# Strictly ordered loads and a new split of the last B matrix in a batched trace-of-product kernel

## The chip, the cores and the metric

The kernel runs on one core of a Trainium2 chip. The profiler's span, from first to last instruction, is 1.7 to 1.8 us shorter than the device time of the same run. Moments such as "at 705.1" are us from the start of the span.

The engines of the core run side by side. In this kernel GpSimd issues the loads, which 16 DMA engines carry out; TensorE transposes and does some products, with its results in a memory called PSUM; VectorE and ScalarE copy and multiply. A pool is a fixed set of buffers, each of which is used again when its last reader is done.

## The reference

```python
def setup_inputs():
    B, N = 8, 2176
    return {"a": np.random.randn(B, N, N).astype(np.float32),
            "b": np.random.randn(B, N, N).astype(np.float32)}

def reference(a, b):
    prod = np.matmul(a, b)
    traces = np.diagonal(prod, axis1=1, axis2=2).sum(axis=-1)
    return traces.astype(np.float32)
```

The trace needs no matrix product: it is the sum over all elements of A transposed times B. Each of the 8 batches is therefore a load of two f32 matrices, a transpose of A and a multiply with a sum. 303 MB are read for eight numbers.

## The kernel before

A matrix has 17 tiles of 128 rows, here simply called rows 0 to 16. A load casts f32 to bf16 on its way and is issued by GpSimd. Loads of four rows are joined in twos, so a batch has two double loads of A, a single one, and the same of B. Double loads share three large buffers, singles two small ones.

```python
    even = [ROWS] * (NT // ROWS) + [1] * (NT % ROWS)
    fine = [4, 4, 4, 2, 1, 1, 1]              # groups of rows of the last B
    LAST_PIECES = [(0, 2), (2, 3), (3, 5)]    # row 16 of the last B comes in three pieces
    stage = ctx.enter_context(tc.tile_pool(name="stage", bufs=3))
    single = ctx.enter_context(tc.tile_pool(name="single", bufs=2))
    ...
    def load(src, start, m, count):
        if m == 1:
            t = single.tile([P, 1, N], bf16, tag="single")
        else:
            t = stage.tile([P, DOUBLE * ROWS, N], bf16, tag="stage")
        ...
        issued = nc.gpsimd.dma_start(out=part, in_=rows)
```

TensorE transposes A into PSUM, ScalarE and VectorE copy it into one large tile `at`, and VectorE multiplies each row of B with its part of `at` and sums along the row, 2.29 us for 2048 columns. In the last batch TensorE takes a part of this: products of 128x128 blocks, summed in PSUM, whose diagonal a multiply with the identity picks out at the very end.

```python
        for start, m, count in joined(b_groups):
            if last and start == N - P:             # row 16 of the last B
                b_t = stage.tile([P, DOUBLE * ROWS, N], bf16, tag="stage")
                row = b_t[:, 0, :]
                for g0, g1 in LAST_PIECES:
                    lo, hi = g0 * WIDE, min(g1 * WIDE, N)
                    nc.gpsimd.dma_start(out=row[:, lo:hi], in_=b[bi, start:start + P, lo:hi])
                ...                                  # split over TensorE and VectorE
                continue
            groups, _ = load(b[bi], start, m, count)
            for start, m, b_t in groups:
                v0 = start // P
                for s in range(m):
                    row = b_t[:, s, :]
                    if last and (m == 1 or s % 2 == 1):
                        half = 2 if m == 1 else 0
                        multiply_on_pe(at, row, v0 + s, half, len(a_groups))
                        if half:
                            on_dve(wide_at(at, v0 + s, 0, half), wide(row, 0, half))
                    else:
                        on_dve(wide_at(at, v0 + s, 0, n_wide), wide(row, 0, n_wide))
                        if last:
                            multiply_on_pe(at, row, v0 + s, n_wide, len(a_groups))
```

The instructions go through a scheduler, which keeps what depends on one another in order but may issue a load ahead of an earlier one whose buffer is not yet free.

## Time and profile before

| | before |
|---|---|
| device time, first three runs | 711.77 us (711.19 to 711.93) |
| span | 709.4 us |
| read from HBM over the span | 427 GB/s |
| VectorE, TensorE, ScalarE busy | 58%, 29%, 28% |
| last piece taken up by TensorE | 705.11 |
| product with the identity (last multiply) | 706.67 |

The page's lines on the DMA engines, the stretches by window and the timeline of the end are shown in the prediction below. How to read them: one digit of the DMA row is a fortieth of the span, 9 standing for 90% busy or more. In a timeline line, the columns are start, duration, engine, source line, operation, what it writes and reads, the count of instructions merged, and in brackets the idle time before it with what ended it.

### The profile page before, as it was taken

How to read it: one execution, taken by the hardware profiler on the slowest of the kernel's cores; microseconds unless marked ns; L12 is line 12 of the kernel's file. 1: busy time of each engine (PE TensorE's matmuls, PEld its weight loads, DVE VectorE, ACT ScalarE, POOL GpSimd, SP SyncE). 2: the span in 40 equal slices, each digit the busy share in tenths (PEclk: the TensorE clock that was granted, in tenths of full speed). 3: DMA queues.
4: the chain of work that ended last, by engine and by line, in shares of the span. 5: the costliest groups of instructions: out<-in, count | busy, mean ns of one | idle time of the engine just before them, and what ended most of it. 6: DMA issues, size and time to landing. Idle time of an engine off the chain costs nothing.

```text
span 709.4 us, 3709 instructions
## 1 busy us (share of the span) xinstructions
PE 206.3 (29%) x1406; PEld 193.0 (27%) x1406; DVE 411.4 (58%) x449; ACT 196.8 (28%) x210; POOL 34.6 (5%) x60
## 2 busy tenths in 40 slices
PE   1542005420065100542006510065100560005655
PEld 0542005410065100541005510065000550005655
DVE  0223996139952399514994259932599335993356
ACT  2443005430064200633006420065200651006610
POOL 1000000000010000100000000000000000000000
PEclk9977557765577655766557665577655775557776
DMA  9999999999999999999999999999999999999996
GB/s 220 220 220 219 206 219 220 219 217 209 219 220 218 217 212 216 220 219 215 212 218 220 218 213 215 215 222 217 215 214 213 225 217 212 215 217 222 219 207 138
DMA packets 11620, 152.32 MB, mean 215 GB/s; under 512 B 850, under 2 KB 1106, under 8 KB 3282
## 3 DMA queue, kind: packets, MB, share of 16 engines
q0 software_dynamic: 11456, 150.97, 100.1%
q1 hardware_dynamic: 146, 1.11, 0.4%
q8 instruction: 11, 0.18, 0.1%
q14 instruction: 7, 0.06, 0.0%
HBM read 303.04 MB, written 0.00 MB: 427 GB/s over the span
## 4 chain that ended last, share of the span: by engine, by line
DMA 56%; DVE 34%; issue 7%; PE 2%; another core or an unknown queue 2%; POOL 0%; DVEq 0%; POOLq 0%
DMA t<-in_b_dram 43%; DVE scratch L122 33%; DMA t<-in_a_dram 13%; PE ps L155 1%; DVE acc L122 0%; DVEq L122 0%; PE ps L176 0%; POOL identity masks.py:199 0%; DVE at L110 0%; POOL identity masks.py:197 0%; PE total L298 0%; DVE result L302 0%; DVE late L122 0%; POOLq L74 0%
## 5 line engine op out<-in xcount | busy, mean ns | idle before, releaser
L122 DVE CUSTOM_DVE_ANT_1 scratch<-at,t 128x2048 bf16<-128x2048 bf16 (+1 forms) x156 | 310.6, 1991 | 74.9 <-DMA t<-in_b_dram 67.7
L112 ACT COPY at<-ps 128x1024 bf16<-128x1024 bf16 x208 | 194.4, 1044 | 474.9 <-PE ps L155 474.5
L155 PE MATMUL ps<-identity,t 128*128 128x128 f32 x1071 | 177.9, 334 | 482.5 <-DVE sums L275 262.7
L155 PEld LDWEIGHTS ps<-identity,t 128*128 128x128 f32 x1071 | 166.2, 213 | 490.8 <-DVE sums L275 311.2
L110 DVE COPY at<-ps 128x1024 bf16<-128x1024 bf16 (+2 forms) x104 | 93.5, 902 | 214.4 <-PE ps L155 196.9
L74 POOL DMA_DIRECT2D t<-in_a_dram x23 | 15.3, 663 | 354.3 <-PE ps L176 156.5
L74 POOL DMA_DIRECT2D t<-in_b_dram x26 | 16.8, 645 | 288.3 <-PE ps L176 147.5
L283 PEld LDWEIGHTS <-at 128*128 128x128 bf16 x153 | 17.1, 122 | 13.3 <-issue 12.7
L283 PE MATMUL trace_ps<-t,at 128*128 128x128 bf16 x144 | 16.7, 293 | 12.3 <-DMA t<-in_b_dram 12.3
L176 PE MATMUL ps<-identity,t 128*128 128x128 bf16 x170 | 16.4, 219 | 4.9 <-DVE at L110 4.8
L176 PEld LDWEIGHTS <-t 128*128 128x128 bf16 x170 | 13.0, 100 | 8.3 <-issue 8.0
L122 DVE DVE_READ_ACCUMULATOR2_ANT acc<- 128x1 f32 x163 | 13.3, 81 | 0.0
L86 DVE CAST t<-words 128x1088 bf16<-128x1088 f32 x1 | 0.7, 726 | 4.8 <-DMA words<-in_a_dram 4.8
L247 POOL DMA_DIRECT2D b_t<-in_b_dram x3 | 1.6, 537 | 16.0 <-DVE acc L122 16.0
L122 DVE CUSTOM_DVE_ANT_0 scratch<-at,t 128x128 bf16<-128x128 bf16 x7 | 2.0, 291 | 0.2
L85 ACT CAST t<-words 128x1088 bf16<-128x1088 f32 x1 | 1.1, 1099 | 3.7 <-DMA words<-in_a_dram 3.7
L122 DVE CUSTOM_DVE_ANT_1 scratch<-at,b_t 128x256 bf16<-128x256 bf16 (+1 forms) x3 | 1.5, 510 | 0.1
L275 DVE TENSOR_REDUCE sums<-acc 128x1 f32<-128x22 f32 (+1 forms) x8 | 1.4, 174 | 0.3
L85 ACT ACT_TABLE_LOAD x1 | 1.3, 1283 | 0.7 <-PEq L321 0.7
L283 PE MATMUL trace_ps<-b_t,at 128*128 128x128 bf16 x9 | 1.3, 284 | 0.4 <-DMA b_t<-in_b_dram 0.4
L298 PE MATMUL total<-late,ones 128*1 128x1 f32 x8 | 0.8, 164 | 0.8 <-DVE late L122 0.8
L298 PEld LDWEIGHTS total<-late,ones 128*1 128x1 f32 x8 | 0.3, 80 | 1.2 <-DVE late L122 1.2
(14 smaller groups left out, 2.7 us busy)
## 6 DMA issues: line engine op xcount, KB each, us to landing
t<-in_a_dram POOLq DMA_DIRECT2D x16, 4352.0 KB, 46.7
t<-in_b_dram POOLq DMA_DIRECT2D x15, 4352.0 KB, 51.5
t<-in_b_dram POOLq DMA_DIRECT2D x9, 544.0 KB, 54.5
t<-in_a_dram POOLq DMA_DIRECT2D x7, 544.0 KB, 53.0
t<-in_b_dram POOLq DMA_DIRECT2D x1, 2176.0 KB, 42.9
words<-in_a_dram SPq DMA_DIRECT2D x1, 1088.0 KB, 4.9
t<-in_b_dram POOLq DMA_DIRECT2D x1, 1088.0 KB, 25.7
b_t<-in_b_dram POOLq DMA_DIRECT2D x1, 256.0 KB, 11.7
```

The lines of the kernel that those rows point to most:

```text
L74: issued = nc.gpsimd.dma_start(out=part, in_=rows)
L85: nc.scalar.copy(out=t[:, 0, :half], in_=plain[:, :half])
L86: nc.vector.tensor_copy(out=t[:, 0, half:], in_=plain[:, half:])
L110: last_copy = nc.vector.tensor_copy(out=dst, in_=src)
L112: nc.scalar.copy(out=dst, in_=src)
L122: nc.vector.tensor_tensor_reduce(out=out, in0=x, in1=y, scale=1.0, scalar=0.0, op0=MUL, op1=ADD, accum_out=acc,)
L155: nc.tensor.transpose(ps[:, n * m + r, :], words[:, r, c0:c0 + step * (P - 1) + 1:step], tiles[f32],)
L176: last_transpose = nc.tensor.transpose(ps16[:, n, r, :], a_t[:, r, c0:c0 + P], tiles[bf16],)
L247: nc.gpsimd.dma_start(out=row[:, lo:hi], in_=b[bi, start:start + P, lo:hi])
L275: nc.vector.reduce_sum(out=tiles["sums"][:, bi:bi + 1], in_=acc[:, :cols], axis=mybir.AxisListType.X)
L283: nc.tensor.matmul(trace_ps, x, y, start=(n == 0), stop=(n == len(pe_work) - 1),)
L298: nc.tensor.matmul(total[:, BATCH - 1:BATCH], tiles["ones"], part, start=(n == 0), stop=(n == len(parts) - 1),)
```

## The change

Its intent: loads land in the order in which they are used, VectorE gets the last B in smaller portions and so starts earlier, TensorE takes four whole rows near the end, and the last tile no longer waits for a large buffer.

```diff
+    PE_ROWS = (11, 12, 13, 15)
-    single = ctx.enter_context(tc.tile_pool(name="single", bufs=2))
+    single = ctx.enter_context(tc.tile_pool(name="single", bufs=3))
+    loaded = []
+    def in_order():
+        return tc.issue_after(loaded[-1].ins) if loaded else nullcontext()
     # in load(), and likewise for the pieces of the last tile:
-        issued = nc.gpsimd.dma_start(out=part, in_=rows)
+        with in_order():
+            issued = nc.gpsimd.dma_start(out=part, in_=rows)
+        loaded.append(issued)
...
-        for start, m, count in joined(b_groups):
+        for start, m, count in ([(*g, 1) for g in b_groups] if last else joined(b_groups)):
             if last and start == N - P:
-                b_t = stage.tile([P, DOUBLE * ROWS, N], bf16, tag="stage")
+                b_t = single.tile([P, 1, N], bf16, tag="single")
...
-                    if last and (m == 1 or s % 2 == 1):
-                        half = 2 if m == 1 else 0
-                        multiply_on_pe(at, row, v0 + s, half, len(a_groups))
-                        if half:
-                            on_dve(wide_at(at, v0 + s, 0, half), wide(row, 0, half))
+                    if last and v0 + s in PE_ROWS:
+                        multiply_on_pe(at, row, v0 + s, 0, len(a_groups))
```

More of the change, by code (lines that the diff above doesn't have):

```diff
@@ L1 @@
 import math
-from contextlib import ExitStack
+from contextlib import ExitStack, nullcontext
 import concourse.bass as bass
@@ L246 @@
                     lo, hi = g0 * WIDE, min(g1 * WIDE, N)
-                    nc.gpsimd.dma_start(out=row[:, lo:hi], in_=b[bi, start:start + P, lo:hi])
+                    with in_order():
+                        loaded.append(nc.gpsimd.dma_start(
+                            out=row[:, lo:hi], in_=b[bi, start:start + P, lo:hi]
+                        ))
                 multiply_on_pe(at, row, v0, 0, 1)
```

## The prediction

> **What bounds the kernel now.** I read the page first: the slices (part 2), the queues and the HBM line, then the stretches by window, then the timeline of the last 50 us.
>
> ```profile
> DMA  9999999999999999999999999999999999999996
> GB/s 220 220 220 219 206 219 220 219 217 209 219 220 218 217 212 216 220 219 215 212 218 220 218 213 215 215 222 217 215 214 213 225 217 212 215 217 222 219 207 138
> ...
> q8 instruction: 11, 0.18, 0.1%
> ...
> HBM read 303.04 MB, written 0.00 MB: 427 GB/s over the span
> ```
>
> The DMA engines are at 90% or more in every slice but the last. The GB/s row counts bytes as written in bf16, half of the f32 bytes read: 427 GB/s of reading is the 215 of the page. All compute engines are far from full (VectorE 58%, TensorE 29%). The bound is the stream of loads; everything else counts only before the stream is full or after its last byte.
>
> ```profile
> core 0: us, PE busy (x) PEld busy (x) DVE busy (x) ACT busy (x) POOL busy (x), PEclk, DMA share, GB/s
> 109.80:197.15 87.35, 23.04 (x153) 21.52 (x153) 54.02 (x59) 24.21 (x26) 3.93 (x7) 0.62 1.02 217
> ...
> 284.54:372.04 87.50, 22.87 (x153) 21.25 (x153) 54.04 (x59) 24.21 (x26) 3.95 (x7) 0.62 1.02 216
> ...
> 692.00:705.10 13.10, 9.12 (x78) 8.76 (x78) 9.69 (x12) 0.00 (x0) 1.51 (x3) 0.61 0.91 181
> 705.10:709.40 4.30, 1.25 (x13) 0.64 (x12) 1.76 (x9) 0.00 (x0) 0.00 (x0) 0.76 0.00 0
> ```
>
> One batch takes 87.4 us with its order of loads either A, A, single (the 109.80 stretch) or A, single, A (the 284.54 stretch): GpSimd's own timeline shows both orders, 87.35 against 87.50. After 705.10 nothing is loaded, and 4.3 us remain.
>
> GpSimd's timeline in the batch before the last, and the whole timeline around the start of the last B:
>
> ```profile
> 614.16 0.70 POOL L74 DMA_DIRECT2D t<-in_a_dram  x1 [26.70 <-DMA t<-in_b_dram]
> 634.62 0.71 POOL L74 DMA_DIRECT2D t<-in_b_dram  x1 [19.76 <-DVE acc L122]
> ```
>
> ```profile
> 675.10 0.36 DVE L110 COPY at<-ps 128x384 bf16<-128x384 bf16 x1 [0.88 <-PE ps L176]
> ...
> 681.89 2.29 DVE L122 CUSTOM_DVE_ANT_1 scratch<-at,t 128x2048 bf16<-128x2048 bf16 x1 [6.42 <-DMA t<-in_b_dram]
> ...
> 691.92 1.59 POOL L247 DMA_DIRECT2D b_t<-in_b_dram  x3 [16.03 <-DVE acc L122]
> ```
>
> And the timeline of the end:
>
> ```profile
> 703.51 1.22 DVE L122 CUSTOM_DVE_ANT_1 scratch<-at,t 128x1024 bf16<-128x1024 bf16 x1
> ...
> 704.86 0.68 DVE L122 CUSTOM_DVE_ANT_1 scratch<-at,b_t 128x512 bf16<-128x512 bf16 x1
> 705.11 0.45 PE L283 MATMUL trace_ps<-b_t,at 128*128 128x128 bf16 x3 [0.41 <-DMA b_t<-in_b_dram]
> ...
> 706.05 0.42 DVE L122 CUSTOM_DVE_ANT_1 scratch<-at,b_t 128x256 bf16<-128x256 bf16 x1
> ...
> 706.67 0.29 DVE L122 CUSTOM_DVE_ANT_0 scratch<-identity,trace_ps 128x128 bf16<-128x128 f32 x1 [0.18 <-DVE late L122]
> ```
>
> Here is the only slack that a change can take. The last piece lands at 705.1 (TensorE starts on it at 705.11 and is done at 705.56), but VectorE is still behind: it works on rows of earlier loads until 704.8, then does its three short products one after the other and reaches the product with the identity, the last real step, at 706.67. TensorE has waited 1.1 us for it.
>
> **What the Trainium skill says.** "DMA: Bandwidth & Descriptors", section "Where 436 GB/s comes from", puts the ceiling of a core's 16 engines at 435.2 GB/s. The trace agrees and shows how near it is: a batch reads 2 x 8 x 2176 x 2176 x 4 / 8 = 37.88 MB in 87.4 us, 433 GB/s. The same page, "Anatomy of one DMA — SWDGE (gpsimd) path", says that DMA engines never wait on semaphores; the issuing sequencer waits, and the engines drain what was queued. So a late issue costs only if the queue runs dry. The trace agrees: GpSimd waits up to 30 us at a time while the DMA row stays at 9. "Runtime: NRT & Kernel Launch", section "Instruction fetch mechanics", says that instructions come in blocks of 16 KiB, 256 instructions, by DMA: the 11 packets with 0.18 MB of q8 fit.
>
> **The change, part by part.**
> (1) Strict order of the loads, with a third small buffer. Comparing the instruction orders of the two kernels: GpSimd's list differs from the fourth batch on, where the single A tile no longer overtakes the second double; no load is added there, and no new wait on a landing of the load before appears. Could the queue run dry? At 614.16 the second A is issued; the second B double has just landed (VectorE starts on it at 614.11), and a B single and an A double are still queued. A double takes (87.4 / 34 rows) x 8 = 20.6 us, a single 2.57: 23 us of work. The single that used to lie there too is 2.6 us of it. Next, B is issued at 634.6 with over 20 us queued. So: 0 us in the middle. At the last batch the second A double lands 2.6 us earlier, as the single now follows it; its transposes (661.3 to about 673.5) and the last copies (675.46) move to about 672.9.
>
> (2) The last B in fours. The first four rows land at about 705.1 - 13 x 2.57 = 671.7, not with the double at 681.8; the others at 682.0, 692.2, then 697.4 (two), 699.9, 702.5 and the pieces at 703.7, 704.3, 705.1. VectorE does rows 0 to 10 and 14, twelve, where it did seven and two halves. Steps of 2.29 us plus the reading of the accumulator, 9.5 us for four (681.89 to 691.39): from 672.9 to 682.4; 682.4 to 691.9; three from 692.3 to 699.4; row 14 from 700.0 to 702.4. It keeps level and is idle when the first piece lands. One more load in the stream: below 0.1 us.
>
> (3) Four full rows on TensorE. Matmuls of L283 fall from 153 to 89 (4 x 17, 12 ends of the other rows, 9 of the last). Row 15 lands at 702.5; 17 at 0.114 us (8.21 / 72) end at 704.5, the first piece's four at 705.0, two more at 705.2, the last three at 705.6: as before.
>
> (4) The last tile in the small pool. Its pieces no longer wait for the first double (691.92); in their place they queue behind the two-row load, which waits for the first four rows to be read, about 682.5. Ten us of loads are then still queued, as there were in the kernel before. Gain 0, since the pieces' turn in the stream is the same.
>
> The end: products of the pieces at 703.8 to 704.5, 704.5 to 705.0, and the last at 705.2 to 705.7; the product with the identity, after TensorE at 705.6 and VectorE at 705.7, starts at about 705.85 in place of 706.67. **Sum: -0.8 us**, all behind the last landing. 711.77 - 0.8 = 711.0; I take 710.9, as the program also shrinks by 128 TensorE instructions, half a fetched block, which uses a DMA engine.
>
> **Rivals.**
> (a) Strict order makes a new stall: the second A and the single behind it, both waiting for VectorE, starve the stream. For it: GpSimd waits 26.7 us there, in order, so one late buffer holds all loads behind it. Against: 23 us are queued, and the second and third batches already run in that order at 87.35 us. Losing 3 us in each of five batches would give 726.
> (b) VectorE becomes the bound of the end: 9.5 us for four rows against 10.3 us of loading is a thin margin. If its start stays at 675.5, it ends the third group at 701.8 and row 14 at 704.2; then the pieces' products end 0.5 us late and nearly all is lost: 711.6. A reader should note that it does more work at the end, yet earlier.
> (c) The 16 DMA engines don't end together: in the last 13.1 us the share is 0.91 and the rate 181, where 1.02 and 217 are usual, about 1.4 us per engine on the mean. If a fetch or a changed order falls on another engine, the last landing moves by some tenths, up to 1 us either way: 710 to 712.
> (d) Strict order raises the rate itself. The dips in the GB/s row, 206 to 213, recur once a batch; were they due to the order, they would differ between the two orders, and they don't: 87.35 and 87.50. At most 5 x 0.15 = 0.7 us: 710.2.
>
> **Range and chances.** Runs of the kernel before spread over 0.7 us, (c) adds some tenths, and (b) and (d) pull apart: 709.9 to 711.9. Faster by 2% would be 697.5 us; 303.04 MB at 435.2 GB/s alone take 696.3 us, and the start, the 3.5 us of end and the 1.7 us between span and time come on top: 0.01. Slower by 2% needs (a) in full: 0.02. Within 2%: 0.97.
>
> **What would show it.** Right: batches of 87.4 us in all windows; the first VectorE product of the last batch at 673 with four rows done by 682.5; the two-row load issued near 682.5; no VectorE product of a whole row running when the first piece lands; the product with the identity 0.7 to 0.9 us after the last landing, not 1.56; last landing 705.1 within 0.5; L283 89 matmuls. Wrong: a slice in the middle under 200 GB/s; a last landing over 1 us away; VectorE still in row 14 at 704; or TensorE ending well after 705.7.

## More of the kernel before

The metric is device time in microseconds (us), the median of several runs.

The loads of the last B in the kernel before, as GpSimd issued them (timeline of GpSimd from 649):

```profile
649.10 1.10 POOL L74 DMA_DIRECT2D t<-in_b_dram  x2 [13.77 <-PE ps L176]
674.06 0.53 POOL L74 DMA_DIRECT2D t<-in_b_dram  x1 [23.86 <-PE ps L176]
675.36 0.53 POOL L74 DMA_DIRECT2D t<-in_b_dram  x1 [0.77 <-PE ps L176]
```

The built program tells which loads they are: at 649.10 rows 8 to 11 together with row 14, at 674.06 rows 12 and 13, at 675.36 row 15. Row 14 is ahead of 12 and 13.

## The result, and the profile after

The changed kernel takes 710.49 us (median of 6 runs, 710.38 to 710.69); the kernel before took 711.25 us in the runs that now stand beside it (6 runs, 711.05 to 711.93, the first three among them). The two ranges don't overlap. Ratios here are the mean time of one kernel's runs over that of the other's of the same rounds, so not quite the ratio of the medians: 0.9988, 95% interval 0.9975 to 1.0. That is 0.85 us of 711, the same at the 2% mark. The upper end of the interval is 1.0, so the times alone only just show a gain; the trace has to say where it is.

From the page of the changed kernel, its DMA rows, its instruction queue and the HBM line:

```profile
DMA  9999999999999999999999999999999999999997
GB/s 220 220 220 214 209 221 220 219 210 213 223 219 213 214 218 220 219 211 214 220 220 216 212 216 220 217 214 214 220 220 215 213 217 219 217 216 214 217 215 143
...
q8 instruction: 10, 0.16, 0.1%
...
HBM read 303.04 MB, written 0.00 MB: 428 GB/s over the span
```

The stream of loads is as full as before, dips included; one block of instructions fewer is fetched (10, not 11). GpSimd's timeline in the seventh and eighth batch:

```profile
547.27 0.70 POOL L83 DMA_DIRECT2D t<-in_b_dram  x1 [19.17 <-DVE acc L132]
...
614.24 1.27 POOL L83 DMA_DIRECT2D t<-in_a_dram  x2 [30.53 <-DVE acc L132]
634.70 0.54 POOL L83 DMA_DIRECT2D t<-in_b_dram  x1 [19.19 <-DVE acc L132]
```

The single of A now goes out behind the second double (x2 at 614.24). From the first B load of one batch to that of the next are 634.70 - 547.27 = 87.43 us; the kernel before had 634.62 - 547.19 = 87.43. The window lengths in the prediction are such distances too, cut at issues of B (109.79, 197.15, 284.54, 372.04); a window's own length proves nothing. Nothing was gained or lost in the middle. The end, in the timeline of all engines:

```profile
672.44 0.36 DVE L120 COPY at<-ps 128x384 bf16<-128x384 bf16 x1 [0.87 <-PE ps L186]
672.72 2.28 DVE L132 CUSTOM_DVE_ANT_1 scratch<-at,t 128x2048 bf16<-128x2048 bf16 x1
...
682.64 1.59 POOL L83 DMA_DIRECT2D t<-in_b_dram  x3 [10.71 <-DVE acc L132]
684.21 1.62 POOL L258 DMA_DIRECT2D b_t<-in_b_dram  x3
...
700.13 2.29 DVE L132 CUSTOM_DVE_ANT_1 scratch<-at,t 128x2048 bf16<-128x2048 bf16 x1 [0.88 <-DMA t<-in_b_dram]
...
702.60 2.07 PE L293 MATMUL trace_ps<-t,at 128*128 128x128 bf16 x17 [1.15 <-DMA t<-in_b_dram]
...
703.79 0.69 DVE L132 CUSTOM_DVE_ANT_1 scratch<-at,b_t 128x512 bf16<-128x512 bf16 x1 [1.16 <-DMA b_t<-in_b_dram]
...
705.41 0.43 DVE L132 CUSTOM_DVE_ANT_1 scratch<-at,b_t 128x256 bf16<-128x256 bf16 x1 [0.42 <-DMA b_t<-in_b_dram]
...
706.02 0.29 DVE L132 CUSTOM_DVE_ANT_0 scratch<-identity,trace_ps 128x128 bf16<-128x128 f32 x1 [0.18 <-PE total L308]
```

VectorE begins on the last B at 672.72, right after the last copy. It is level with the loads by the third group, for which it waits from 691.55 to 692.29. Row 14 (700.13), the first piece (703.79) and the last (705.41) are waits on a DMA too, and the second piece is taken up at 704.55, 0.13 us after it landed. In the kernel before, VectorE came late to all three pieces. The multiply with the identity starts at 706.02 instead of 706.67.

### The profile page after: what moved, and what is told of

It is laid out like the page before. It is cut to its first block, busy times and chain, and to the rows that moved or that the text cites. A ratio compares the mean times of both kernels' runs of the same rounds, so it can differ in the third digit from the quotient of the medians.

```text
span 708.7 us, 3573 instructions
## 1 busy us (share of the span) xinstructions
PE 197.8 (28%) x1342; PEld 184.2 (26%) x1342; DVE 420.6 (59%) x455; ACT 196.8 (28%) x210; POOL 35.0 (5%) x61
## 4 chain that ended last, share of the span: by engine, by line
DMA 54%; DVE 29%; another core or an unknown queue 10%; PE 3%; issue 2%; ACT 1%; POOL 1%; DVEq 0%; POOLq 0%
DMA t<-in_b_dram 42%; DVE scratch L132 29%; DMA t<-in_a_dram 12%; PE ps L165 2%; ACT at L122 1%; POOL t L83 1%; PE trace_ps L293 0%; DVE acc L132 0%; DVEq L132 0%; PE ps L186 0%; POOL identity masks.py:199 0%; DVE at L120 0%; PE total L308 0%; POOL identity masks.py:197 0%
## 5 line engine op out<-in xcount | busy, mean ns | idle before, releaser
L132 DVE CUSTOM_DVE_ANT_1 scratch<-at,t 128x2048 bf16<-128x2048 bf16 (+1 forms) x159 | 319.6, 2010 | 76.7 <-DMA t<-in_b_dram 69.4
L293 PE MATMUL trace_ps<-t,at 128*128 128x128 bf16 x80 | 9.6, 290 | 22.7 <-DMA t<-in_b_dram 22.3
L293 PEld LDWEIGHTS <-at 128*128 128x128 bf16 x89 | 9.8, 122 | 23.6 <-issue 22.9
```

Source lines behind the costliest of these rows:

```text
L132: nc.vector.tensor_tensor_reduce(out=out, in0=x, in1=y, scale=1.0, scalar=0.0, op0=MUL, op1=ADD, accum_out=acc,)
L293: nc.tensor.matmul(trace_ps, x, y, start=(n == 0), stop=(n == len(pe_work) - 1),)
```

## The experiments

The intervals of the ratios are about 0.13% wide on each side, 0.9 us, so times alone don't tell most of these kernels from one another. The traces do, with one profiled execution for each kernel: in each I read the last landing and the start of the multiply with the identity, and their distance is what compute still costs after the stream has ended. A load leaves 16 completion records in the trace, and it has landed with the last of them; no printed view shows these records.

| kernel | time, us (runs) | ratio to before (95%) | last landing | identity product | distance |
|---|---|---|---|---|---|
| before | 711.25 (6) | | 705.07 | 706.67 | 1.60 |
| changed | 710.49 (6) | 0.9988 (0.9975 to 1.0) | 705.28 | 706.02 | 0.74 |
| e1, order alone | 710.79 (5) | 0.9992 (0.9979 to 1.0004) | 705.33 | 706.49 | 1.16 |
| e9, order in the last B alone | 710.53 (5) | 0.9989 (0.9976 to 1.0001) | 705.21 | 706.08 | 0.87 |
| e3, changed with old rows | 710.65 (5) | 0.9991 (0.9978 to 1.0003) | 705.03 | 706.17 | 1.14 |
| e2, changed without order | 717.05 (4) | 1.0079 (1.0064 to 1.0095) | 705.42 | 712.65 | 7.23 |
| e4, changed without fours | 716.86 (2) | 1.0075 (1.0056 to 1.0093) | 705.57 | 712.66 | 7.09 |
| e8, last tile in large pool | 711.97 (5) | 1.0007 (0.9994 to 1.002) | 706.69 | 707.43 | 0.74 |
| e12, a fetch put back | 710.67 (5) | 0.9989 (0.9976 to 1.0001) | 705.19 | 706.38 | 1.19 |
| e5, row 12 on VectorE | 710.51 (4) | 0.9984 (0.9969 to 0.9999) | 705.28 | 706.04 | 0.76 |
| e6, rows 12 and 15 on VectorE | 712.96 (2) | 1.002 (0.9991 to 1.005) | not needed | 708.42 | |
| e11, two large buffers | 734.27 (2) | 1.032 (1.0283 to 1.0357) | not needed | | |

The kernel before had medians of 711.31 to 711.43 us beside the experiments. All outputs were correct.

### e1 and e9: which part brings the gain?

The prediction booked 0 on the order and the whole gain on the fours and the rows. But the order of issue above suggested a rival: row 14 lands ahead of rows 12 and 13, which are used first. e1 adds to the kernel before nothing but `in_order()`; e9 adds it only within the last B:

```diff
+        return tc.issue_after(loaded[-1].ins) if at_end else nullcontext()
...
             groups, _ = load(b[bi], start, m, count)
+            at_end = last
```

> The kernel before with nothing but the strict order of loads (two small buffers, double load in the last B, old split of rows, last tile in the large pool). Theory P, which is how the prediction booked the gain: order gives 0, the gain comes from the fours and the rows on TensorE, so the time is that of before, 711.3 us within 0.2, and the product with the identity starts about 1.5 us after the last landing. Rival O: the gain comes from the order at the very end alone. In the kernel before, the single load of row tile 14 goes out ahead of the load of tiles 12 and 13, so tile 12 reaches VectorE 2.6 us late (699.9) and pushes two half rows in front of the last pieces; in order it would land near 697.3, and VectorE would be level with the loads (12 from 697.4 to 699.8, half of 14 from 700.0, half of 15 from 702.6 to 703.8). Then this run is 0.7 to 0.8 us faster than before, 710.5, with the identity product 0.8 us after the last landing.

> The kernel before with only the loads of the last B held in order: against before, one pair of loads changes places, the single of row tile 14 and the load of tiles 12 and 13; all loads up to the last B stay as they were, singles overtaking. Theory P: 711.3 us, as before. Rival O: 710.5 us, as the whole strict order, because only this one pair matters. If e1 gains and this doesn't, the gain lies in the middle of the run, against both.

The first line is VectorE in the kernel before, taking up row 12:

```profile
699.91 2.29 DVE L122 CUSTOM_DVE_ANT_1 scratch<-at,t 128x2048 bf16<-128x2048 bf16 x1 [3.09 <-DMA t<-in_b_dram]
```

VectorE in e9, row 12, the halves of rows 14 and 15, and the identity:

```profile
697.39 2.29 DVE L131 CUSTOM_DVE_ANT_1 scratch<-at,t 128x2048 bf16<-128x2048 bf16 x1 [0.50 <-DMA t<-in_b_dram]
...
699.97 1.23 DVE L131 CUSTOM_DVE_ANT_1 scratch<-at,t 128x1024 bf16<-128x1024 bf16 x1 [0.28 <-DMA t<-in_b_dram]
...
702.94 1.22 DVE L131 CUSTOM_DVE_ANT_1 scratch<-at,t 128x1024 bf16<-128x1024 bf16 x1 [1.73 <-DMA t<-in_b_dram]
...
706.08 0.29 DVE L131 CUSTOM_DVE_ANT_0 scratch<-identity,trace_ps 128x128 bf16<-128x128 f32 x1 [0.18 <-PE total L311]
```

With one pair of loads exchanged, row 12 starts 2.5 us earlier, and the second half row ends at 704.2 instead of 704.7. That is still 0.4 us after the first piece has landed (703.80), but row 15 itself landed some 0.3 us late in e9 (see e12). In the kernel before VectorE stood idle for 3.09 us at 697 to 700, with row 14 already there, and then had 4.8 us of work in one piece (699.91 to 704.7), part of it in front of the pieces. e9 has nearly the whole gain in time and 0.73 of the 0.86 us in distance. So the order brings nearly all of the gain, and only at the end. e1 agrees in kind (VectorE takes row 12 at 697.56 there), but its distance is 1.16, not the 0.8 expected; e12 below is about that rest.

### e3: the old split of rows in the changed kernel

```diff
-                    if last and v0 + s in PE_ROWS:
-                        multiply_on_pe(at, row, v0 + s, 0, len(a_groups))
+                    if last and (m == 1 or s % 2 == 1):
+                        half = 2 if m == 1 else 0
+                        ...    # as in the kernel before
```

> The changed kernel with the old split of rows (odd rows of the groups and halves of the two single tiles on TensorE, 153 products there in place of 89). Theory P: fours and rows act together through VectorE being level with the loads; with fours and old rows VectorE has even less to do, so it stays at 710.5 us, within 0.15 of the changed kernel. Rival O: the same 710.5. A rival that books the gain on TensorE's fewer matmuls says 711.0 or more. It tells whether part (3) is worth anything by itself.

The time, 710.65, is within noise of the changed kernel, so this run doesn't tell the theories apart. In the trace, fours bring nothing beyond the order: the distance is 1.14, like e1. The new rows bring some tenths in the trace, if anything.

### e2 and e4: what the parts are worth together

e2 takes only the order out of the changed kernel (`in_order()` always returns `nullcontext()`); e4 takes only the fours out (`joined(b_groups)` for the last B too).

> The changed kernel without the strict order (third small buffer, fours, four rows on TensorE and the small last tile kept). By the order of issue of the built program, the three pieces of the last tile and both singles now overtake the load of tiles 12 and 13, which lands last. TensorE takes its products in program order, so 34 for 12 and 13, 1, 17 for row 15 and 9 for the pieces, 61 at 0.115 us or 7.0 us, start after the last landing near 705.2, in place of 3. End of TensorE about 712.3, where it was 705.8: about 6.4 us slower than the changed kernel, 717 us. If order only mattered for VectorE it would be 711.3; if order didn't matter at all, 710.5.

> The changed kernel with the first eight rows of the last B in one double load again. It lands at 682.0, and VectorE has eight rows at 2.36 us to do at once: until 700.9, rows 8 to 10 until 708.0, 14 until 710.3, then 0.2 for the sum and 1.9 for the pieces, identity product about 712.5 in place of 706.0: 717 us. If fours are worth nothing, 710.5. With e3 it tells that fours and rows belong together: the new split of rows needs the fours, the old one doesn't.

The end of e2, in the timelines of GpSimd, TensorE and VectorE, and last VectorE's multiply with the identity in e4:

```profile
678.27 1.59 POOL L258 DMA_DIRECT2D b_t<-in_b_dram  x3 [0.77 <-PE ps L186]
688.22 0.54 POOL L83 DMA_DIRECT2D t<-in_b_dram  x1 [8.35 <-issue]
```

```profile
705.47 6.06 PE L293 MATMUL trace_ps<-t,at 128*128 128x128 bf16 x52 [5.45 <-DMA t<-in_b_dram]
711.37 1.15 PE L293 MATMUL trace_ps<-b_t,at 128*128 128x128 bf16 x9
```

```profile
712.65 0.29 DVE L132 CUSTOM_DVE_ANT_0 scratch<-identity,trace_ps 128x128 bf16<-128x128 f32 x1 [3.81 <-PE total L308]
```

```profile
712.66 0.29 DVE L132 CUSTOM_DVE_ANT_0 scratch<-identity,trace_ps 128x128 bf16<-128x128 f32 x1 [0.18 <-DVE late L132]
```

Both came out as expected. In e2 the pieces are issued at 678.27 and rows 12 and 13 only at 688.22, behind them. TensorE, which works in program order, has 52 + 9 products still to do after the last landing, and the bound of the end passes from VectorE to TensorE: +6.6 us against the changed kernel. In e4 VectorE has no pause from the landing of the double to the end and reaches the identity at 712.66. So the other parts taken together are safe only with the order, and the new rows only with the fours: leaving out the order or the fours costs more than 6 us, eight times what the whole change gains.

### e5 and e6: how much room VectorE has

`PE_ROWS = (11, 13, 15)` and `PE_ROWS = (11, 13)`.

> The changed kernel with row 12 on VectorE, so 11, 13 and 15 on TensorE. VectorE: 8 to 10 until 699.3, 12 until 701.6, 14 until 704.0, then the three pieces until 705.9, identity product about 706.1 in place of 706.02. Theory (0.9 us of slack before row 14 and 1.2 us after it take up a row of 2.35 us almost whole): 710.5 to 710.7. Rival (VectorE is the bound of the end, each row put back costs 2.35 us): 712.8.

> The changed kernel with rows 12 and 15 back on VectorE, so 11 and 13 on TensorE. In the run with row 12 alone moved, row 14 ended on VectorE at 704.1 where the first piece landed at 703.8: the slack is used up. Row 15 must now cost its full step: 704.1 to 706.4, sum, the three pieces until 708.3, identity product 708.4 in place of 706.0: 712.9 us. If VectorE still had slack, 710.5.

VectorE's multiply with the identity, in e5 and in e6:

```profile
706.04 0.29 DVE L132 CUSTOM_DVE_ANT_0 scratch<-identity,trace_ps 128x128 bf16<-128x128 f32 x1 [0.18 <-PE total L308]
```

```profile
708.42 0.29 DVE L132 CUSTOM_DVE_ANT_0 scratch<-identity,trace_ps 128x128 bf16<-128x128 f32 x1 [0.18 <-DVE late L132]
```

A row of 2.3 us put back costs 0.02 us (706.04 against 706.02), because it fills two waits; the next costs its whole step, 2.38 us. Four rows on TensorE are one more than needed. e5 has the lowest ratio of all, but its runs (710.17 to 710.59) are not told apart from the changed kernel's.

### e8: the last tile in the large pool

```diff
-                b_t = single.tile([P, 1, N], bf16, tag="single")
+                b_t = stage.tile([P, DOUBLE * ROWS, N], bf16, tag="stage")
```

> The changed kernel with the last tile in the large pool again. The three pieces then wait for the second group of four to be read by VectorE, about 691.6, in place of going out at 684.2 right behind the two singles. At 691.6 the loads of rows 12 and 13, 14 and 15 and the end of 8 to 11 are still queued, some 10 us. Theory (an issue costs only if the queue runs dry): 710.5 us, the same as the changed kernel within 0.15, landings of the pieces unmoved. Rival (the small pool matters by itself): the pieces land later, some tenths to 1 us slower.

This was a miss: 711.97 us, about 1.5 us slower than the changed kernel. GpSimd and VectorE in e8:

```profile
701.47 1.60 POOL L258 DMA_DIRECT2D b_t<-in_b_dram  x3 [17.65 <-PE trace_ps L293]
```

```profile
705.19 0.69 DVE L132 CUSTOM_DVE_ANT_1 scratch<-at,b_t 128x512 bf16<-128x512 bf16 x1 [2.75 <-DMA b_t<-in_b_dram]
```

The pieces were not issued at 691.6 but at 701.47. I had assumed that the pool hands out its buffers in turn. The wait listed in the built program is on the load of rows 12 and 13, so the pool gave the last tile their buffer, and TensorE was done with them only at about 701.2. By then the single of row 15 was the only load left (it landed at 702.36). From issue to the first product were 3.7 us, and the stream ran dry: from 700 to 703 us the share of the load queue is 40.1%, where it is 103.1% in the changed kernel. The rule held (a late issue costs only when the queue runs dry); the assumption about the buffer did not. With the new split of rows, the small pool is worth about 1.4 us (707.43 against 706.02).

### e12: the fetch of a block of instructions

In e1, e9 and e3 row 15 landed late, at 702.81 to 703.21, where it landed at 702.56 in the changed kernel. All three fetched a block of instructions at about 701; the changed kernel, with 128 instructions fewer on TensorE, fetched none there. Counted from the landing of rows 12 and 13, row 15 lands 5.25 to 5.28 us later in the five kernels in this order that fetched none there (changed, e4, e5, e6, e8), and 5.58 to 5.83 in these three. e12 adds 76 needless products while TensorE is idle in the seventh batch, which moves the limits of the blocks:

```diff
+        if bi == BATCH - 2:
+            idle = psum_idle.tile([P, P], f32, tag="idle")
+            with tc.issue_after(last_transpose.ins):
+                for n in range(76):
+                    nc.tensor.matmul(idle, tiles[bf16], tiles[bf16], start=True, stop=True)
```

> The changed kernel with 76 needless products of identity with identity added to TensorE's program in the seventh batch, when it is idle, into a tile that nobody reads. In the three runs with 153 products at the end a 16 KiB block of instructions was fetched at 700.8 to 701.2, and the load of row 15 landed 0.3 to 0.6 us late (702.8 to 703.2, against 702.6 in the changed kernel, which has no fetch there: 10 blocks in place of 11). The 152 added instructions should bring the eleventh fetch back to about 701. Theory F (the fetch delays the load in flight, which is what fewer TensorE instructions are worth): row 15 starts on TensorE at 702.9 to 703.2, its end at 706.1, time 710.7 to 710.9. Rival (the late landing came from something else): 702.6 and 710.5 us. The added products themselves cost nothing in either, since TensorE is idle there.

The DMA queues of e12 in the window from 700 to 703 us (packets, MB, share of 16 engines), then TensorE taking up row 15, then the identity:

```profile
q0 software_dynamic: 349, 0.56, 101.8%
q8 instruction: 1, 0.02, 1.9%
```

```profile
703.10 2.12 PE L300 MATMUL trace_ps<-t,at 128*128 128x128 bf16 x17 [1.67 <-DMA t<-in_b_dram]
```

```profile
706.38 0.29 DVE L133 CUSTOM_DVE_ANT_0 scratch<-identity,trace_ps 128x128 bf16<-128x128 f32 x1 [0.62 <-PE total L315]
```

The fetch is back, row 15 starts at 703.10 instead of 702.60 (it lands 5.84 us after rows 12 and 13), and the identity comes 0.36 us later. The next load's landing was not late (first piece 703.69, against 703.77), so it is the completion of the load in flight that is held up, not the stream; only the last of its 16 completion records is clearly out of place (703.06, the one before it at 702.47). In time it is 710.67 against 710.49, at the edge of what runs tell apart, on different occasions; the trace is the evidence. Why the hold-up doesn't carry over to the next load stays open. Nor does every fetch show: the kernel before fetched its eleventh block at 703.28, and its pieces then landed 1.23, 0.61 and 0.81 us after one another, against 1.21, 0.65 and 0.86 in the changed kernel.

### e11: how near the strict order is to an empty queue

`stage` with two buffers in place of three.

> The changed kernel with two large buffers in place of three, to see how near the strict order is to an empty queue in the middle. With two, a double load goes out only when the one before the last has been read: an A double when the first B double has been read (20.4 us after landing, about as the second B double lands), so at its issue little more than a single of 2.6 us is queued, against 23 us with three. Theory (a late issue costs only what the queue runs dry by, some 2 to 4 us between issue and first data against 2.6 us queued): 0 to 1.5 us per batch, 711 to 721 us. If the strict order were near stalling already with three buffers, this would cost far more, 5 us and more per batch, 745 and above.

It took 734.27 us, more than my theory allowed and less than its rival. GpSimd in the fifth batch, and TensorE's start on that load:

```profile
359.68 0.70 POOL L83 DMA_DIRECT2D t<-in_a_dram  x1 [31.52 <-DMA t<-in_b_dram]
```

```profile
385.58 6.57 PE L165 MATMUL ps<-identity,t 128*128 128x128 f32 x32 [57.69 <-DMA t<-in_a_dram]
```

This double load is issued with just a single in the queue and is there 25.9 us later; behind a full queue a double takes 20.6. By this one load, as an estimate, it needs to be issued some 5.3 us before the queue ends, where I had put 2 to 4. It landed some 2.7 us late: at 385.45, where the single had landed at 362.13 and back to back would have been 382.7. Measured so, each A double from the second batch on was 0.4 to 3.1 us late, 19 us in all, and the loads of the last B another 6; these make up the loss. With three buffers 23 us lie in the queue at the tightest issue, and the strict order is far from that.

## Why the prediction was right or wrong

**The time** was right: 710.9 predicted, 710.49 measured, within the range, with a gain of 0.8 us predicted and 0.85 measured by the ratio. The end of the changed kernel ran step by step as described, but which part earned the gain was booked wrongly (steps 1 and 2), so the right sum is no proof of the shares in it. The bound was the one named: the stream of loads, untouched, with only the end to be had.

**Step (1), strict order: 0 us.** Right for the middle: 87.43 us from batch to batch in both kernels. The last copies moved from 675.46 to 672.80 as said. But wrong at the end: the step looked at the A tiles only and missed that in the last B the single of row 14 overtook rows 12 and 13. e9 shows that this one pair of loads is nearly the whole gain. The landings that step (2) lists are in order (12 and 13 at 697.4, 14 at 699.9), so the order was in the sum all along, under another name.

**Step (2), fours: VectorE keeps level.** Its working was right to some tenths of a us: first product at 672.72 (672.9 said), row 14 from 700.13 (700.0 said), idle when the first piece lands. What was wrong is the credit. With the order alone, the old split in one double keeps nearly level as well (e9: a distance of 0.87, against 0.74). The fours are needed only because of the new rows (e4).

**Step (3), four rows on TensorE.** 89 products, as said, and no cost: TensorE ends at 705.8 (705.6 said). The half block of instructions, which the prediction let count for next to nothing, is what this part brings: against the old rows in the same order, a fetch less at 701, and 0.40 to 0.45 us less distance in the trace (e3, e12).

**Step (4), small pool: 0.** The pieces were issued at 684.21, at the place in the stream that was said. But e8 shows the alternative was not as harmless as the kernel before made it look: about 1.4 us.

**The end.** The identity was predicted at 705.85 and came at 706.02, with the last landing 0.2 us later than before.

**The rivals.** (a), a stall: none; e11 shows how it would have looked. (b), VectorE as the bound: not in the changed kernel, since its start did move to 672.7; e5 and e6 show that the thin margin was one row wide. (c), last landing moved by tenths: 705.03 to 705.57 over all kernels except e8 (706.69) and the two that were not read; its reason stays open. Fetches don't explain it: the four kernels with a fetch near 701 lie at 705.03 to 705.33, inside that range. (d), a higher rate by order: not seen, 215 GB/s mean in both pages.

## What to carry to other kernels

When the loads bound a kernel, look at the last ones in the order in which they were issued, not in the order of the program: a scheduler may let a small load overtake, which costs nothing while the stream runs and something at its end. Read for each engine whether it waits for data after the last landings or still has old work; only old work can be removed. And test the parts of a change against each other: here one pair of loads made nearly all of the gain, and the other parts, taken together, are harmless only in its company.

## What the Trainium skill lacked or had wrong

- "Runtime: NRT & Kernel Launch", "Instruction fetch mechanics", calls the cost of crossing a 16 KiB block "mostly hidden". What it costs the engine was not measured here; but the fetch is itself a DMA, and a single load in flight landed 0.3 to 0.6 us late in the four kernels with a fetch at about 701 (TensorE on row 15 at 703.10 against 702.60 in e12). The fetch at 703.28 in the kernel before delayed no landing.
- "DMA: Bandwidth & Descriptors", "Anatomy of one DMA — SWDGE (gpsimd) path", gives about 2.0 us of fixed cost per DMA. In e11 a double load of 4352 KB, issued when the single before it had 2.45 us left to land, landed 2.7 us later than back to back; by an estimate from the page's 2.0 us, those 2.45 us would have covered it. The 256 KB piece in e8 took 3.7 us from issue to use, near the estimate of 3.2 that the page's formula gives for its 524 KB of f32.
- The same page, "Where 436 GB/s comes from", says that in transfers between HBM and SBUF the HBM limit of about 358 GB/s binds. This core, alone, read 427 GB/s over the whole span. The note under "Measured (HBM→SBUF, 128 partitions, SWDGE, issued from GpSimd)" on that page puts 358 at both cores of a pair streaming, which no run here tested, so the sentence needs that condition.
- No page that I read says how far the 16 engines drift apart in a long stream. In the kernel before, the 16 completion records of a load lie 0.45 us apart at 46 us, 1.58 at 68, after the first block of instructions was fetched at 51.64, and 2.65 for the last piece (702.42 to 705.07). From 692.00 to 705.10 the mean share of the engines is 0.91, after 1.01 to 1.02. What moves them apart was not tested.
